# Small float32 products of a block, alternating between tiles of the TensorE array

## The chip, the cores and the metric

The kernel runs on one core of a Trainium2 chip. The core has TensorE (PE), which multiplies, VectorE (DVE), ScalarE (ACT), GpSimd (POOL) and SyncE (SP), whose queue issues most of the transfers from memory. The metric is the time of one execution in device microseconds.

## The reference

Two transformer blocks in float32, one after the other, on 512 tokens of width 1024. The change touches the first block alone:

```python
mod = (silu(c) @ w_ada + b_ada)                 # 1024 x 6144: six vectors, shift, scale and gate of both halves
h = rms_norm(x) * (1 + scale1) + shift1
gq, gk, gv, gz, ga, gb, sq, sk, sv = split(h @ w_in)
# gated delta rule, 8 heads of 64, chunks of 64 tokens
A = where(strict, (kb @ k.T) * decay, 0);  L = A + eye
u, w = solve(L, [v * beta, kb * exp(G)])        # unit lower triangular, 64 x 64
qk = where(causal, (q @ k.T) * decay, 0)
# over the chunks: v_new = u - w S;  o = q_dec S + qk v_new;  S = S * dec + k_dec.T v_new
# sliding window attention, 8 query heads on 2 key heads, window 128, blocks of 128 queries
s = (q @ k.T) / 8 - slope * dist;  p = exp(s - m) / (sum + exp(sink - m));  o = p @ v
x = x + gate1 * (concat(o_g, o_s) @ w_out)
x = x + gate2 * ffn(rms_norm(x) * (1 + scale2) + shift2)
```

## The kernel before

Activations lie transposed, 128 features by 512 tokens in a tile. Large products go through `mm3` (L299): both operands are split into a high and a low part of a faster float32 format, and three products are summed. The small products that the change touches are plain float32, and each is two records of TensorE in the trace. A scheduler sets each engine's order ahead of time; a call under `tc.high_priority` pulls its work forward. On the chip every engine then keeps to its order.

*Modulation.* `w_ada` is read in 16 parts: eight of 256 columns for the first two vectors (`adaln1`, early), eight of 512 (`adaln2`, groups g = 0 to 7) later. `gemv` (L330) makes eight products of a part, the padded vector as weights (32 columns), the matrix as data. The output of product k lies in the 32 partitions from 32 * (k % 4), so four products use four column tiles, and the second four add to the first. `columns` (L337) sums the rows by products with a vector of ones. ADA_AT places the groups: g = 4 and 5 at the turns ADA_AT[2] of the last stage, where their matrix goes through the slots of x4 and x5, two loads of 256 KB at a time (`ring_x`).

*Keys, Gram matrices, inverse.* Heads go by pairs; e, the parity, is the head of the pair that lies in partitions 0 to 63 (e = 0) or 64 to 127. A block b is 128 tokens, two chunks. `key_products` (L729) makes k k^T of four heads of one parity in a PSUM bank, before the stage. `inverse(b)` (a generator of three steps) makes q k^T the same way (L789) and takes the inverse of the 64x64 triangles from inverses of smaller blocks, in two levels; each level is two groups of four products of 128x128x128 (L797 and L802, L811 and L817), with two VectorE operations of 128x512 (L799, L803) or four ScalarE copies behind them. The 128x128 matrices hold two chunks on the diagonal; off it there is nothing that matters.

*Recurrence.* `recur(b)` takes u and w (L857, L862, L865), products with the state (L829), outputs (L893), and the state update (L873), eight products that alternate between two column tiles; `outputs(b)` norms and transposes them (L909).

*Attention.* `swa_scores(b, kv)` makes the scores of four query heads with key head kv (L1005, array rows 64 * kv on), the bias and maximum on VectorE (L1009, L1014), exps (L1021) and scalings (L292) on ScalarE. `swa_values(b, kv)` transposes (L1040), copies (L1042) and multiplies (L1044) into one bank, and ScalarE copies the result into the query tiles x0 to x3 (L1047).

*The order around the change.* The loop over TURNS runs the steps of `inverse`, and after the third `recur` and `outputs`, all under high priority; at each turn n it first calls `swa_step(n)`: the scores of unit n and the values of unit n - 1. Free places on TensorE are filled by products of lower priority, at the end by those of the output projection (`out_proj`, ps_out). The slots x4 and x5, and the others, are loaded again with x for it (L1120), and the result of each group is added to them (L1111), which frees one of three banks.

## Time and profile before

| | us |
|---|---|
| three runs | 1289.23, 1296.19, 1282.57 (median 1289.23) |
| the profiled execution | 1288.95 |
| its span | 1287.2 |
| TensorE busy | 1260.0 (98%) |
| VectorE busy | 788.7 (61%) |
| ScalarE busy | 507.6 (39%) |
| mean granted clock of TensorE | 0.986 |

The span goes from the first to the last instruction. Engines work side by side, so the busy times are no sum. A busy share is an average over stages with different limits; the prediction reads single stages. The granted clock is the share of full speed that the chip gave TensorE; here it stands at 1.0 or at 0.5.

### The profile page before, as it was taken

What the parts mean: (1) busy time and instruction counts of PE and PEld (TensorE: products, weight loads), DVE (VectorE), ACT (ScalarE), POOL (GpSimd) and SP (SyncE); (2) the same over time, 40 slices, a digit from 0 to 9 for tenths busy, and PEclk for the clock granted to TensorE, in tenths of its full rate; (3) what the DMA queues carried; (4) which work ended last, traced back from release to release, by engine and by line L of the source; (5) the groups of instructions that cost most, each with busy time, mean ns of one, the idle gap of its engine ahead of it and who ended that gap; (6) DMA issues with size and microseconds to landing.
All of it is one profiled execution on the core that took longest, in us unless ns stands there. A gap on an engine that the chain in (4) does not pass through costs nothing.

```text
span 1287.2 us, 17346 instructions
## 1 busy us (share of the span) xinstructions
PE 1260.0 (98%) x6670; PEld 1015.7 (79%) x6670; DVE 788.7 (61%) x1665; ACT 507.6 (39%) x988; POOL 42.9 (3%) x39
## 2 busy tenths in 40 slices
PE   5999999999999999999999999999999999999997
PEld 3676778767789888888888888888888888788876
DVE  5598758746565744333433336898778876754554
ACT  4456422635345222222322222345544454432342
POOL 1200001000000000000000000021000000000000
PEclk9999999969999999999999999899999999999999
DMA  9534332002430523232233334122222222233441
GB/s 349 205 106 174 131 99 83 17 17 85 142 119 1 196 85 96 99 98 90 87 101 118 114 119 141 50 75 76 79 82 66 66 78 79 76 96 98 133 145 50
DMA packets 52627, 132.64 MB, mean 103 GB/s; under 512 B 6560, under 2 KB 14272, under 8 KB 52544
## 3 DMA queue, kind: packets, MB, share of 16 engines
q1 hardware_dynamic: 49472, 126.21, 30.4%
q10 hardware_dynamic: 3072, 5.33, 1.3%
q8 instruction: 52, 0.85, 0.3%
q14 instruction: 31, 0.25, 0.1%
HBM read 127.30 MB, written 4.21 MB: 102 GB/s over the span
## 4 chain that ended last, share of the span: by engine, by line
PE 93%; DMA 2%; DVE 2%; ACT 1%; issue 1%; DVEq 0%; ACTq 0%; SPq 0%
PE ps_mm L299 63%; PE ps_out L299 3%; PE ps_sm L330 3%; PE ps_ff L299 2%; PE ps_sc L1538 1%; PE ps_po L1044 1%; PE ps_swa L1005 1%; PE ps_o L1568 1%; DMA raw<-in_wo 1%; PE ps_mm L1683 1%; PE ps_mm L1684 1%; PE ps_tr L1562 1%; PE ps_sc L299 1%; PE ps_mm L1682 1%; PE ps_sm L337 1%; PE ps_g L524 1%
## 5 line engine op out<-in xcount | busy, mean ns | idle before, releaser
L280 ACT ACTIVATE whi<-raw 128x1024 fp32r<-128x1024 f32 x141 | 147.4, 1045 | 275.2 <-PE ps_mm L299 209.3
L281 DVE TENSOR_TENSOR wlo<-raw,whi 128x1024 fp32r<-128x1024 f32 x140 | 170.5, 1218 | 100.5 <-ACT whi L280 100.2
L299 PE MATMUL ps_mm<-uh,whi 128*128 128x512 f32 (+1 forms) x544 | 197.6, 363 | 0.0
L299 PE MATMUL ps_mm<-uh,wlo 128*128 128x512 f32 (+1 forms) x544 | 197.0, 362 | 0.4 <-DVE work L1272 0.4
L299 PE MATMUL ps_mm<-ul,whi 128*128 128x512 f32 (+1 forms) x544 | 195.7, 360 | 0.0
L299 PE MATMUL ps_mm<-mh,whi 128*128 128x512 f32 x320 | 126.3, 395 | 0.0
L299 PE MATMUL ps_mm<-ml,whi 128*128 128x512 f32 x320 | 125.5, 392 | 0.0
L299 PE MATMUL ps_mm<-mh,wlo 128*128 128x512 f32 x320 | 125.2, 392 | 0.0
L299 PEld LDWEIGHTS ps_mm<-ul,whi 128*128 128x128 f32 x544 | 102.8, 189 | 15.7 <-issue 0.7
L299 PEld LDWEIGHTS ps_mm<-uh,whi 128*128 128x128 f32 x544 | 102.6, 189 | 15.7 <-issue 1.5
L299 PEld LDWEIGHTS ps_mm<-uh,wlo 128*128 128x128 f32 x544 | 102.6, 189 | 15.6 <-DVE work L1272 0.7
L299 PEld LDWEIGHTS ps_mm<-ml,whi 128*128 128x128 f32 x320 | 60.0, 188 | 14.2
L299 PEld LDWEIGHTS ps_mm<-mh,wlo 128*128 128x128 f32 x320 | 60.0, 188 | 13.7
L299 PEld LDWEIGHTS ps_mm<-mh,whi 128*128 128x128 f32 x320 | 59.9, 187 | 13.4
L299 PE MATMUL ps_mm<-ah,whi 128*128 128x512 f32 x176 | 69.8, 396 | 0.0
L299 PE MATMUL ps_mm<-al,whi 128*128 128x512 f32 x176 | 69.8, 396 | 0.0
L299 PE MATMUL ps_mm<-ah,wlo 128*128 128x512 f32 x176 | 69.8, 396 | 0.0
L299 PE MATMUL ps_mm<-hh,wlo 128*128 128x512 f32 x144 | 58.3, 405 | 0.0
L299 PE MATMUL ps_mm<-hh,whi 128*128 128x512 f32 x144 | 57.8, 401 | 0.0
L299 PE MATMUL ps_mm<-hl,whi 128*128 128x512 f32 x144 | 57.7, 400 | 0.0
L1186 DVE SCALAR_TENSOR_TENSOR fa<-th,ps_mm 128x512 f32<-128x512 f32 x20 | 13.7, 687 | 58.9 <-ACT th L1184 58.9
L1586 DVE TENSOR_TENSOR work<-ps_mm,rstd 128x512 f32<-128x512 f32 x32 | 22.0, 689 | 45.1 <-PE ps_mm L299 44.9
(559 smaller groups left out, 2418.7 us busy)
## 6 DMA issues: line engine op xcount, KB each, us to landing
raw<-in_win SPq DMA_DIRECT2D x80, 512.0 KB, 3.6
ada<-in_ada SPq DMA_DIRECT2D x48, 256.0 KB, 5.9
raw<-in_wgate SPq DMA_DIRECT2D x22, 512.0 KB, 3.6
raw<-in_wup SPq DMA_DIRECT2D x22, 512.0 KB, 3.5
ada<-in_ada SPq DMA_DIRECT2D x16, 512.0 KB, 4.1
raw<-in_wdown SPq DMA_DIRECT2D x16, 512.0 KB, 3.5
x<-in_xT SPq DMA_DIRECT2D x16, 256.0 KB, 4.0
raw<-in_wout SPq DMA_DIRECT2D x8, 512.0 KB, 3.4
```

Of the source, the lines that this page charges most:

```text
L280: S.activation(out=hi[:, 0:n, :], in_=raw[:, 0:n, :], func=AF.Copy)
L281: eng.tensor_tensor(out=lo[:, 0:n, :], in0=raw[:, 0:n, :], in1=hi[:, 0:n, :].bitcast(F32), op=ALU.subtract)
L299: E.matmul(dst, ww[:, k, :], xx, start=first and i == 0, stop=last and i == len(seq) - 1)
L330: E.matmul(pt[j:j + 32, :], cpad[:, k // 2, k % 2:k % 2 + 32], src, start=k < 4, stop=k >= 4, tile_position=(0, j))
L337: E.matmul(pt[:, j:j + 1], acc[:, j * P:(j + 1) * P], ones[:, 0:1], start=True, stop=True)
L524: E.transpose(dst[:, b * P:(b + 1) * P], src[:, b * P:(b + 1) * P], ident)
L1005: E.matmul(pp[:, f + c0_:f + 256], qsT[j][o:o + 64, b * P:(b + 1) * P], ksT[o:o + 64, k0:(b + 1) * P], start=True, stop=True)
L1044: E.matmul(po_[o:o + 64, :], Vs[:, kblk * P + o:kblk * P + o + 64], pT, start=kb == kbs[0], stop=kb == 1)
L1186: V.scalar_tensor_tensor(out=fa, in0=th, scalar=1.0, in1=pg, op0=ALU.add, op1=ALU.mult)
L1538: E.matmul(pt[:, 0:w], xx[:, sl_], kk[:, c], start=q == 0, stop=q == 2)
L1562: E.transpose(pt[0:nk, i * P:(i + 1) * P], pv(i, c), ident)
L1586: pump(V.tensor_tensor(out=gt, in0=pt, in1=rstd[:, c], op=ALU.mult))
```

## The change

Products that use different parts of the array are put next to each other. In `gemv` the first of each four products also waits for the last load of the four; ADA_AT[2] goes from turns 3 and 6 to 5 and 7, and `ring_x` takes x4, x5 and x6, x7 by turns. Key products and q k^T alternate between the parities, with both banks open. Each 128-wide product of the inverse becomes two 64-wide ones on the diagonal, which alternate; L799 and L803 go by halves. Scores alternate between the key heads, the values of both follow each other, and a turn makes either the scores of a block or its values. Lines of the program move by some twenty: L729 becomes L738, L789 L809, L797 to L817 become L792, L829 L850, L873 L894, L1005 L1026, L1040 L1060, L1044 L1066, L330 L335, L337 L344, L299 L300, L1111 L1136, L1120 L1145, L376 (the loads of `adaln2`) L382.

```diff
-ADA_AT = (2, (3, 4), (3, 6))
+ADA_AT = (2, (3, 4), (5, 7))
...
+    def together(first, last):
+
+        tc.add_manual_dep(first.ins, last.ins.name, SYNC, reason="products side by side")
+
+    def gemv(how, acc, views, loads=()):
 
 
         n = acc.shape[1]
...
         pt = psum("sm")[:, 0:n]
         for k, src in enumerate(views):
             j = 32 * (k % 4)
-            E.matmul(pt[j:j + 32, :], cpad[:, k // 2, k % 2:k % 2 + 32], src, start=k < 4, stop=k >= 4, tile_position=(0, j))
+            ins = E.matmul(pt[j:j + 32, :], cpad[:, k // 2, k % 2:k % 2 + 32], src, start=k < 4, stop=k >= 4, tile_position=(0, j))
+            if k % 4 == 0:
+                together(ins, loads[k // 4])
...
+        views, loads = [], []
         for i in range(4):
             src = A["ada2"][g, i].rearrange("p a b -> p (a b)")
             raws = ring()
             w = 2 * T // len(raws)
             for n, raw in enumerate(raws):
-                nc.sync.dma_start(out=raw, in_=src[:, n * w:(n + 1) * w])
+                ins = nc.sync.dma_start(out=raw, in_=src[:, n * w:(n + 1) * w])
                 views += [raw[:, j:j + T] for j in range(0, w, T)]
+            if i % 2:
+                loads.append(ins)
         acc = accp.tile([P, T], F32, tag="acc", name="acc", bufs=2)
-        gemv(how, acc, views)
+        gemv(how, acc, views, loads)
...
-    def key_products(b, e):
-
-        at = Zf[b, e]
-        o, sl_ = 64 * e, slice(b * P, (b + 1) * P)
+    def key_products(b):
+
+        sl_ = slice(b * P, (b + 1) * P)
         kk = []
 
-        def part(q):
-            if q == 0:
-                kk.append(psum("blk"))
+        def part(q, e):
+            if q + e == 0:
+                kk.extend(psum("blk") for _ in range(2))
                 for i in range(4):
-                    E.matmul(kk[0][:, i * P:(i + 1) * P], kT[i][o:o + 64, sl_], kT[i][o:o + 64, sl_], start=True, stop=True)
+                    for d in range(2):
+                        k_ = kT[i][64 * d:64 * d + 64, sl_]
+                        E.matmul(kk[d][:, i * P:(i + 1) * P], k_, k_, start=True, stop=True)
+            at = Zf[b, e]
...
-        fill.extend(lambda q=q: part(q) for q in range(4))
+        fill.extend(lambda q=q, e=e: part(q, e) for e in range(2) for q in range(4))
...
+        stream = "g" if b == 0 else "inv"
+        ends = (slice(0, 64), slice(64, P))
+
+        def products(dst, left, right):
+
+            for q in range(4):
+                for r in ends:
+                    c = slice(q * P + r.start, q * P + r.stop)
+                    E.matmul(dst[r, c], left[r, c], right[r, c], start=True, stop=True)
+
...
-            qk = psum("g" if b == 0 else "inv")
-            for q in range(4):
-                E.matmul(qk[:, cs[q]], kT[q][o:o + 64, s], qT[q][o:o + 64, s], start=True, stop=True)
-            V.tensor_tensor(out=dt, in0=qk, in1=dt, op=ALU.mult)
+        qk = [psum(stream) for _ in range(2)]
+        for q in range(4):
+            for e in range(2):
+                o = 64 * e
+                E.matmul(qk[e][:, cs[q]], kT[q][o:o + 64, s], qT[q][o:o + 64, s], start=True, stop=True)
+        for e in range(2):
+            dt = qkT[b, e]
+            V.tensor_tensor(out=dt, in0=qk[e], in1=dt, op=ALU.mult)
...
-            pp = psum("g" if b == 0 else "inv")
-            for c in cs:
-                E.matmul(pp[:, c], at[e][:, c], x[e][:, c], start=True, stop=True)
+            pp = psum(stream)
+            products(pp, at[e], x[e])
             pj = tmp_tile(b)
-            V.tensor_tensor(out=a3(pj), in0=a3(pp), in1=bcm(cc("lev", P)), op=ALU.mult)
-            pz = psum("g" if b == 0 else "inv")
-            for c in cs:
-                E.matmul(pz[:, c], pj[:, c], z[:, c], start=True, stop=True)
-            V.tensor_tensor(out=z, in0=z, in1=pz, op=ALU.subtract)
+            for r in ends:
+                V.tensor_tensor(out=a3(pj)[r, :, r], in0=a3(pp)[r, :, r],
+                                in1=bcm(cc("lev", P))[r, :, r], op=ALU.mult)
+            pz = psum(stream)
+            products(pz, pj, z)
+            for r in ends:
+                V.tensor_tensor(out=a3(z)[r, :, r], in0=a3(z)[r, :, r], in1=a3(pz)[r, :, r], op=ALU.subtract)
...
-    def swa_scores(b, kv):
-
-        o = 64 * kv
+    def swa_scores(b):
+
         c0_ = 0 if b else P
-        sc = sw.tile([P, 4, 256], F32, tag="sc", name="sc", bufs=2)
+        sc = [sw.tile([P, 4, 256], F32, tag="sc", name="sc", bufs=2) for _ in range(2)]
+        k0 = (b - 1) * P if b else 0
         for jj in range(2):
-            pp = psum("swa")
+            pp = [psum("swa") for _ in range(2)]
             for j in (2 * jj, 2 * jj + 1):
                 f = (j % 2) * 256
-                k0 = (b - 1) * P if b else 0
-                E.matmul(pp[:, f + c0_:f + 256], qsT[j][o:o + 64, b * P:(b + 1) * P], ksT[o:o + 64, k0:(b + 1) * P],
-                         start=True, stop=True)
+                for kv in range(2):
+                    o = 64 * kv
+                    E.matmul(pp[kv][:, f + c0_:f + 256], qsT[j][o:o + 64, b * P:(b + 1) * P], ksT[o:o + 64, k0:(b + 1) * P],
+                             start=True, stop=True)
...
-    swa_po = [None]
-
-    def swa_values(b, kv, sc):
-        o = 64 * kv
-        if kv == 0:
-            swa_po[0] = psum("po")
-        po_ = swa_po[0]
+    def swa_values(b, sc):
+        po_ = psum("po")
         kbs = (0, 1) if b else (1,)
         for kb in kbs:
-            pp = psum("swa")
-            for j in range(4):
-                E.transpose(pp[:, j * P:(j + 1) * P], sc[:, j, kb * P:(kb + 1) * P], ident)
-            pT = sw.tile([P, T], F32, tag="pT", name="pT", bufs=2)
-            S.activation(out=pT, in_=pp, func=AF.Copy)
-            kblk = b - 1 + kb
-            E.matmul(po_[o:o + 64, :], Vs[:, kblk * P + o:kblk * P + o + 64], pT, start=kb == kbs[0], stop=kb == 1)
-        if kv == 1:
-            for j in range(4):
-                S.activation(out=qsT[j][:, b * P:(b + 1) * P], in_=po_[:, j * P:(j + 1) * P], func=AF.Copy)
-
-    swa_units = [(b, kv) for b in range(NB) for kv in range(2)]
+            pT = []
+            for kv in range(2):
+                pp = psum("swa")
+                for j in range(4):
+                    E.transpose(pp[:, j * P:(j + 1) * P], sc[kv][:, j, kb * P:(kb + 1) * P], ident)
+                pT.append(sw.tile([P, T], F32, tag="pT", name="pT", bufs=2))
+                S.activation(out=pT[kv], in_=pp, func=AF.Copy)
+            for kv in range(2):
+                o = 64 * kv
+                c = (b - 1 + kb) * P + o
+                E.matmul(po_[o:o + 64, :], Vs[:, c:c + 64], pT[kv], start=kb == kbs[0], stop=kb == 1)
+        for j in range(4):
+            S.activation(out=qsT[j][:, b * P:(b + 1) * P], in_=po_[:, j * P:(j + 1) * P], func=AF.Copy)
+
     swa_sc = []
 
     def swa_step(n):
 
-        if n < len(swa_units):
-            swa_sc.append(swa_scores(*swa_units[n]))
-        if n:
-            swa_values(*swa_units[n - 1], swa_sc[n - 1])
+        if n % 2 == 0:
+            swa_sc.append(swa_scores(n // 2))
+        else:
+            swa_values(n // 2, swa_sc[n // 2])
 
...
-    ring_x = lambda: [xtile(4), xtile(5)]
+    ring_n = [0]
+
+    def ring_x():
+        ring_n[0] += 1
+        return [xtile(6), xtile(7)] if ring_n[0] % 2 == 0 else [xtile(4), xtile(5)]
...
-        if n <= len(swa_units):
+        if n < 2 * NB:
```

TensorE's order in the middle of the stage, before. L797 to L817 are groups of the inverse, L1005 scores and L1044 values of the attention, L893 and L873 the recurrence:

```order
L811 MATMUL ps_inv<-h_2177,Z 128x128 x4
L1044 MATMUL ps_po<-pT,Vs 64x512
L1005 MATMUL ps_swa<-ksT,x_1797 128x256
L1005 MATMUL ps_swa<-ksT,x_1853 128x256
L1005 MATMUL ps_swa<-ksT,x_1685 128x256
L1005 MATMUL ps_swa<-ksT,x_1741 128x256
L817 MATMUL ps_inv<-h_2175,blank 128x128 x4
L817 MATMUL ps_inv<-h_2185,blank 128x128 x4
L893 MATMUL ps_so<-vn,qkT 128x64 x8
L873 MATMUL ps_rec<-vn,Kt 64x64 x8
L802 MATMUL ps_inv<-h_2503,l_2789 128x128 x4
```

The same place in the change:

```order
L792 MATMUL ps_inv<-h_2223,blank 64x64 x8
L792 MATMUL ps_inv<-h_2227,blank 64x64 x8
L850 MATMUL ps_rec<-St,kT 128x64 x4
L1066 MATMUL ps_po<-pT,Vs 64x512
L1026 MATMUL ps_swa<-ksT,x_1685 128x256 x2
L1026 MATMUL ps_swa<-ksT,x_1741 128x256 x2
L792 MATMUL ps_inv<-h_2579,l_2885 64x64 x8
L850 MATMUL ps_rec<-St,kT 128x64
L930 MATMUL ps_so<-cst,on 128x128 x4
```

A group of four became one of eight in the same places, scores of a query tile come in pairs (one for each key head), and the values product of this block still stands alone.

TensorE's order at the end of the stage, in the change. L1060 are the transposes of the last attention block, L930 the last of the recurrence, L335 the eight modulation products of g = 5:

```order
L1060 MATMUL ps_swa<-cst,sc 128x128 x4
L930 MATMUL ps_so<-cst,on 128x128 x4
L1066 MATMUL ps_po<-pT,Vs 64x512 x2
L335 MATMUL ps_sm<-x_2843,cpad 32x512
L335 MATMUL ps_sm<-x_2844,cpad 32x512
L335 MATMUL ps_sm<-x_2847,cpad 32x512
L335 MATMUL ps_sm<-x_2848,cpad 32x512
L335 MATMUL ps_sm<-x_2851,cpad 32x512
L335 MATMUL ps_sm<-x_2852,cpad 32x512
L335 MATMUL ps_sm<-x_2855,cpad 32x512
L335 MATMUL ps_sm<-x_2856,cpad 32x512
L344 MATMUL ps_sm<-ones,acc 128x1 x4
```

Before, these eight stood one by one among output products, all of them ahead of the last values products. Now the output products go on behind L344.

SyncE's order there, in the change; x_2851 to x_2856 take the same slots as x_2843 to x_2848, and x_3334 (slot x4) is the first one that the output needs:

```order
L277 DMA raw<-in_wgate 128x1024
L277 DMA raw<-in_wup 128x1024
L382 DMA x_2851<-in_ada 128x512
L382 DMA x_2852<-in_ada 128x512
L382 DMA x_2855<-in_ada 128x512
L382 DMA x_2856<-in_ada 128x512
L1145 DMA x_3330<-in_xT 128x512
L1145 DMA x_3331<-in_xT 128x512
L1145 DMA x_3332<-in_xT 128x512
L1145 DMA x_3333<-in_xT 128x512
L277 DMA raw<-in_wgate 128x1024
L1145 DMA x_3334<-in_xT 128x512
```

Before, the loads of the x tiles were spread over this stretch, two of them among the loads of g = 4; now all of them come behind the last four loads of g = 5.

## Rows read from the trace of the kernel before

**Rows 1.** The page's busy line: engine, us (share of the span), instructions.
```profile
PE 1260.0 (98%) x6670; PEld 1015.7 (79%) x6670; DVE 788.7 (61%) x1665; ACT 507.6 (39%) x988; POOL 42.9 (3%) x39
```

**Rows 2.** Table of stretches: us, busy time (instructions) by engine, granted clock, DMA.
```profile
198.80:367.00 168.20, 166.97 (x1133) 127.17 (x1133) 105.50 (x280) 73.95 (x215) 7.42 (x6) 0.93 0.21 70
...
254.50:278.50 24.00, 23.47 (x108) 15.54 (x108) 11.07 (x33) 5.83 (x14) 0.00 (x0) 0.50 0.00 1
...
250.00:260.00 10.00, 8.97 (x64) 7.16 (x64) 7.89 (x28) 8.17 (x23) 0.00 (x0) 0.73 0.01 2
```

**Rows 3.** TensorE's waits: line, releaser: us in total, times, longest.
```profile
PE ps_sm L330 <- DMA ada<-in_ada: 10.5, 1, 10.5
...
PE ps_out L299 <- DVE x L1111: 1.7, 1, 1.7
...
PE ps_rec L857 <- DVE fs L902: 0.5, 1, 0.5
```

**Rows 4.** TensorE's order of time: start, us, line, records; modulation products.
```profile
88.09 1.07 PE L330 MATMUL ps_sm<-ada,cpad 128*32 128x512 f32 x8
...
330.06 1.05 PE L330 MATMUL ps_sm<-x,cpad 128*32 128x512 f32 x2
```

**Rows 5.** TensorE by line, 190 to 385 us: records | busy us, mean ns.
```profile
L1044 PE MATMUL ps_po<-pT,Vs 128*64 128x512 f32 x28 | 17.0, 710 | 0.0
L1005 PE MATMUL ps_swa<-ksT,x 64*128 64x256 f32 x48 | 14.6, 440 | 0.0
L330 PE MATMUL ps_sm<-x,cpad 128*32 128x512 f32 x32 | 12.1, 604 | 0.0
...
L789 PE MATMUL ps_inv<-qT,kT 64*128 64x128 f32 x48 | 7.1, 286 | 0.0
...
L789 PE MATMUL ps_g<-qT,kT 64*128 64x128 f32 x16 | 2.3, 285 | 0.0
```

**Rows 6.** TensorE by line, 22 to 196 us.
```profile
L330 PE MATMUL ps_sm<-ada,cpad 128*32 128x512 f32 x64 | 14.8, 605 | 0.0
...
L729 PE MATMUL ps_blk<-kT 64*128 64x128 f32 x64 | 7.8, 293 | 0.0
```

**Rows 7.** TensorE's order of time: inverse, state update, 64-wide products, values.
```profile
294.59 1.16 PE L797 MATMUL ps_inv<-l,Z 128*128 128x128 f32 x8
295.58 1.06 PE L817 MATMUL ps_inv<-h,blank 128*128 128x128 f32 x8
...
247.90 0.69 PE L873 MATMUL ps_rec<-vn,Kt 128*64 128x64 f32 x16
248.52 1.16 PE L802 MATMUL ps_inv<-h,l 128*128 128x128 f32 x8
...
309.61 1.02 PE L865 MATMUL ps_rec<-tt,h 64*64 64x64 f32 x14
...
311.85 1.93 PE L1044 MATMUL ps_po<-pT,Vs 128*64 128x512 f32 x4
```

**Rows 8.** TensorE's order of time: products of different array rows.
```profile
284.42 0.27 PE L789 MATMUL ps_inv<-qT,kT 64*128 64x128 f32 x1
284.42 0.27 PE L829 MATMUL ps_rec<-St,kT 64*128 64x64 f32 x1
```

**Rows 9.** VectorE and ScalarE by line, 190 to 370 us.
```profile
L799 DVE TENSOR_TENSOR l<-ps_inv,csta 128x512 f32<-128x512 f32 x6 | 4.1, 677 | 1.9 <-PE ps_inv L797 1.9
...
L831 DVE TENSOR_TENSOR on<-ps_so,egc 128x256 f32<-128x256 f32 x6 | 2.5, 422 | 6.6 <-PE ps_so L829 6.5
...
L1021 ACT ACTIVATE sc<-sc,smx 128x256 f32<-128x256 f32 x24 | 11.9, 497 | 4.6 <-DVE smx L1017 4.5
...
L1047 ACT ACTIVATE x<-ps_po 128x128 f32<-128x128 f32 x16 | 3.1, 284 | 6.9 <-PE ps_po L1044 6.9
```

**Rows 10.** DMA issues: queue, count, KB each, median us from issue to landing.
```profile
x<-in_xT SPq DMA_DIRECT2D x16, 256.0 KB, 4.0
...
x<-in_ada SPq DMA_DIRECT2D x16, 256.0 KB, 2.7
```

More of the change, by code (lines that the diff above doesn't have):

```diff
@@ L356, in ada1_load @@
             t = early.pop(0)
-            nc.sync.dma_start(out=t, in_=A["ada1"][k, i])
-            raws.append(t)
+            raws.append((t, nc.sync.dma_start(out=t, in_=A["ada1"][k, i])))
         return raws
     def adaln1(k, raws):
-        views = [raws[kk // 2][:, kk % 2 * 2 * P:kk % 2 * 2 * P + 2 * P] for kk in range(KD)]
+        views = [raws[kk // 2][0][:, kk % 2 * 2 * P:kk % 2 * 2 * P + 2 * P] for kk in range(KD)]
         acc = accp.tile([P, T], F32, tag="acc", name="acc", bufs=2)[:, 0:2 * P]
-        gemv("E", acc, views)
+        gemv("E", acc, views, [raws[3][1]] * 2)
         columns(acc, k, 8, 2)
     def adaln2(g, how, ring):
-        views = []
+        views, loads = [], []
         for i in range(4):
@@ L808, in inverse @@
             z = a3(Zi[b, e])
-            pp = psum("g" if b == 0 else "inv")
-            for c in cs:
-                E.matmul(pp[:, c], at[e][:, c], x[e][:, c], start=True, stop=True)
+            pp = psum(stream)
+            products(pp, at[e], x[e])
             pj = blank[e]
@@ L814, in inverse @@
                 S.activation(out=a3(pj)[o + 32:o + 64, :, o:o + 32], in_=a3(pp)[o + 32:o + 64, :, o:o + 32], func=AF.Copy)
-            pz = psum("g" if b == 0 else "inv")
-            for c in cs:
-                E.matmul(pz[:, c], pj[:, c], Zi[b, e][:, c], start=True, stop=True)
+            pz = psum(stream)
+            products(pz, pj, Zi[b, e])
             for o in (0, 64):
@@ L939, in build @@
     for b in range(NB):
-        for e in range(2):
-            key_products(b, e)
+        key_products(b)
     rest = [lambda: values(0)] + [lambda p=p, f=f: f(p) for p in range(1, 4) for f in (queries, values)]
@@ new lines, in swa_scores @@
+        for kv in range(2):
+            sm = gs.tile([P, 4, 4], F32, tag="smx", name="smx", bufs=2)
+            mx, es, dn, nm = [sm[:, i, :] for i in range(4)]
+            V.tensor_reduce(out=mx, in_=sc[kv][:, :, c0_:256], axis=AX.X, op=ALU.max)
+            V.tensor_tensor(out=mx, in0=mx, in1=cc("slope", 4, 4 * kv), op=ALU.mult)
+            V.tensor_tensor(out=mx, in0=mx, in1=rows[:, 16 + 4 * kv:20 + 4 * kv], op=ALU.max)
+            V.tensor_scalar(out=nm, in0=mx, scalar1=-1.0, scalar2=None, op0=ALU.mult)
+            V.tensor_tensor(out=es, in0=rows[:, 16 + 4 * kv:20 + 4 * kv], in1=mx, op=ALU.subtract)
+            S.activation(out=es, in_=es, func=AF.Exp)
+            for j in range(4):
+                S.activation(out=sc[kv][:, j, c0_:256], in_=sc[kv][:, j, c0_:256], func=AF.Exp, scale=2.0 ** -(4 * kv + j + 1),
+                             bias=nm[:, j:j + 1], accum_out=dn[:, j:j + 1])
+            V.tensor_tensor(out=dn, in0=dn, in1=es, op=ALU.add)
+            V.reciprocal(out=dn, in_=dn)
+            for j in range(4):
+                scale_by(sc[kv][:, j, c0_:256], dn[:, j:j + 1])
```

35 lines of the change are left out of this document (11 added, 24 removed).

## The prediction, made before the changed kernel ran

> **What bounds the kernel now.** I read the page's busy line first: TensorE 1260.0 of a span of 1287.2 us, 98%, VectorE 61%; the chain of waits then, which runs over TensorE almost throughout [rows 1]. So time comes off only where TensorE has less to do, and it comes off one for one until another engine is late. All that the change touches lies before 385 us; from there on TensorE's order is the same in both kernels. The table of stretches shows the stage that matters, 198.8 to 367.0 us: TensorE busy 166.97 of 168.20, VectorE 105.50, ScalarE 73.95, and inside it 24.00 us at a granted clock of 0.50, the lower of the two levels (1.2 GHz; elsewhere 2.4) [rows 2]. The third row says what TensorE did around the fall: in 250 to 260 it was busy 8.97 of 10.00 [rows 2], among short products, with a wait of 0.5 us on VectorE [rows 3]. The profiled execution took 1288.95 us, 0.3 below the median 1289.23 of the three runs (1282.57 to 1296.19); the sum is made against 1288.95.
>
> **What comes off TensorE.**
>
> (a) *Modulation products.* A group of four products in four 32-wide column tiles already stands side by side in places, and then eight records take 1.07 us; a single product, two records, takes 1.05 [rows 4]. So a group of four costs what one costs. The 96 records of 512 columns are 14.8 and 12.1 us of busy time [rows 5, 6]: 48 products, in the change 12 groups of four. 12 x 1.0 = 12.0, saving 14.9; some of the busy time is a pipelined tail under the next instruction, so I take 14. The 256-column ones at the start wait for their loads (10.5 us in one wait [rows 3]); that they now wait for the last of four I cost at 0, since the loads pace them either way (bounds -1.5 and +1.5).
>
> (b) *Inverse.* A group of four 128-wide products takes 0.99 us from start to start (294.59 to 295.58); 32 groups, 31.7. In the change each is eight 64-wide products, alternating between two tiles. The nearest row is the state update L873, eight such products alternating between two tiles: 247.90 to 248.52, 0.62 for 16 records. 64-wide products in one tile take 1.02 for 14 [rows 7]. 32 x 0.62 = 19.8: saves 11.9. If the two tiles don't overlap, 16 records at 1.02/14 are 1.17, and the term is a loss of 5.8.
>
> (c) *Gram and key products.* 7.1 + 2.3 us (64 records) and 7.8 us (64) [rows 5, 6]. That products of the lower and the upper 64 rows of the array run at once the trace shows: at 284.42 one of either kind starts in the same record time [rows 8]. Halved, that is 8.6 off; groups keep their own switch-over, and I take 6 (bounds 0 and 8.6).
>
> (d) *Attention scores.* 14.6 us for the 48 records of 256 columns [rows 5], some of it at half clock; halved, 7.3 off; I take 5.5, since a pair keeps its switch-over (bounds 0 and 7.3).
>
> (e) *Attention times values.* 28 records, 17.0 us, 14 products [rows 5]. In the new order only three of the seven pairs stand next to each other; the others still have transposes between. A pair saves one product, two records at 0.43 (four of them take 1.93 at 311.85 [rows 7]): 3 x 0.86 = 2.6.
>
> Gross: 14 + 11.9 + 6 + 5.5 + 2.6 = 40.
>
> **What is given back.**
>
> (f) *VectorE in the stage.* Each of 16 inverse operations of 128x512 (677 ns) becomes two of half the partitions and half the elements. The time goes by elements per partition: 128x256 takes 422 ns [rows 9]. So +16 x (0.84 - 0.68) = +2.6 us of VectorE. That alone lay beside TensorE before; the cover shrinks. Of the 40 us about 31 come off this stage (the key products and eight of the twelve groups of (a) lie ahead of it), so TensorE has some 136 us left there against VectorE's 108, and less than that before the tail: 159 output products stood before the last attention product in the old order, 72 do in the new. Two engines that feed each other at such a ratio wait for each other: bounds 0 (all overlaps) and 20 (they take turns in one block of the four after another); I take 5, nearer to the few waits that the trace shows [rows 3] than to the other end.
>
> (g) *The stage's tail.* Before, the last group of modulation products was strung out as singles among output products (as at 330.06), x4 and x5 were reloaded long before use, and one wait of 1.7 us on the output eviction stayed [rows 3]. Now (second pair of orders) its two groups of four stand at the end of the stage with no other product between or behind. Step by step: the transposes of block 3 wait for the exps and scalings of both heads, ScalarE 8 x 0.50 for the exps [rows 9] and as much for scalings of the same shape, 8 us in a row where half of it was before, of which I let 3 show; the first group's bank is that of the values and waits for its four copies, 4 x 0.28 = 1.1 [rows 9]; the second group's loads are issued only once the first group's products have read the slots, 2.7 to landing [rows 10] and the issue of four in a row, which I put at 4.1 together; then the first output product needs a bank that is freed by an eviction on x4, whose reload starts when the second group has read x4: 4.0 [rows 10] plus 0.9 for issue and eviction, less the 2 that the group's end and its columns fill, 2.9. Together 11.1; the old 1.7 goes: 9.4 (bounds 3 and 16, by half or twice the latencies).
>
> (h) *Clock.* The fall to 1.2 GHz costs 12 us now (24.00 us of work at half rate [rows 2]). The change has more short products and more waits, so a fall is as likely as before; I leave it at 12, net 0 (bounds -12, none, and +24, two more of the same length).
>
> **Sum:** 40 - 5 - 9.4 = 25.6 off 1288.95: 1263.4, so about **1264 us**.
>
> **A rule against (b).** No row of before has two tiles of different array rows writing one PSUM bank; L873's tiles differ in columns, the products of [rows 8] go to different banks. The inverse writes both diagonal tiles into one bank, at different partitions. If such writes took turns, (b) would be between 0 and its loss of 5.8, the gross 26, and the time 1288.95 - 26 + 14.4 = 1277. I give it 0.1: in L873 two tiles write one bank at different partitions and overlap [rows 7], and the diagonal tiles also write different partitions. The Trainium skill, TensorEngine Tiling (Array Packing), section Gotcha 1: PSUM Pressure, states that different row tiles cannot use the same PSUM bank at one time; that is the case just worked out, and no row here shows it either way.
>
> **The rivals.**
>
> *VectorE and ScalarE become the bound* (0.18). For it: at most 136 against 108 us in the stage, softmax of both heads at once on ScalarE. If (f) is 15 and (g) 13, the sum is -40 + 28 = 1277; with one more fall of the clock of 6 us, 1283. Against: VectorE's instructions are spread over the stage, and TensorE waits on it for less than 2 us of 168 now. The same page of the Trainium skill, section PSUM Bottleneck, says that faster tiles can leave the PSUM copy as the bottleneck; [rows 2] bear it out only as a possibility.
>
> *More than the sum* (0.18). The tail is covered better than I read (3 instead of 9.4) and (c), (d) reach their halves: 1252; if the clock does not fall in the stage, 1240.
>
> *Slower: the clock* (0.07). It fell near a wait of 0.5 us among short products. The change makes such waits frequent from 200 to 330 us. If the lower level holds most of the stage, 100 us instead of 24, TensorE's work takes 38 us longer again: 1264 + 38 = 1302, and with (f) at 15, 1312. It decides from about 75 us more at half clock. Against: before, the clock came back after 24 us with no other change than that TensorE no longer waited (23.47 us busy of 24.00 [rows 2]).
>
> *It doesn't do what it says* (0.05): alternating products run one after another throughout. Then (a) remains, since [rows 4] has it, (b) is -5.8, (c) to (e) are 0: -14 + 5.8 + 9.4 gives 1290.
>
> **Numbers.** The forecast's own case (1256 to 1272) has 0.42, the one-bank rule 0.10, VectorE and ScalarE 0.18, more 0.18, the clock 0.07, no overlap 0.05. A measurement tells about 1%, 13 us: faster is below 1276, slower above 1302. Faster: 0.42 + 0.18, half of the one-bank case (0.05) and a third of the VectorE case (0.06), 0.71. Slower: the clock case, 0.07. Same: the rest, 0.22. The range takes in the VectorE and the one-bank case above, and of "more" all but the case without a fall of the clock: 1245 to 1287.
>
> **What would show it.** (b): the products of L792 start in pairs, a group in about 0.62 us; 1.0 or more says the one-bank rule. (a): groups of eight L335 records in 1.0. (c), (d): two records of L809 or L1026 in the time of one. (f): TensorE's busy share from 200 to 330 us, now above 0.98, at 0.95 or so, with VectorE as the releaser; below 0.88 is the rival. (g): waits of TensorE on x<-in_ada (about 4 us) and on the eviction L1136 (about 3) just after the last values product. (h): one stretch of about 24 us at 0.50, no more. The prediction is wrong if the order that both kernels share after 385 us starts less than 15 or more than 40 us earlier.

## The result, and the profile after

The changed kernel takes 1295.68 us (median of 19 runs, 1289.88 to 1301.86) against 1288.66 before (19 runs): a ratio of 1.0061, 95% interval 1.0044 to 1.0078. It is 0.6% slower, less than the 1% that the prediction took as no change, and outside its range of 1245 to 1287. Runs over 1.5% above the fastest of their kernel, two of inv_serial and one of no_swa below, are left out of the ratios.

The page of the changed kernel; its busy line answers to [rows 1], and the last line is the granted clock in 40 slices.

```profile
span 1291.6 us, 17879 instructions
...
PE 1236.5 (96%) x6926; PEld 1007.6 (78%) x6926; DVE 789.8 (61%) x1681; ACT 507.4 (39%) x988; POOL 42.5 (3%) x39
...
PEclk9999998779889999999999999899999999999999
```

TensorE is busy 23.5 us less and the span is 4.4 longer. The table of stretches of the changed kernel (us, then busy time of PE, PEld, DVE, ACT, POOL, granted clock, DMA), with the stretch that also stands for the experiments in the first row:

```profile
200.00:340.00 140.00, 122.40 (x1182) 96.70 (x1177) 97.73 (x261) 65.27 (x197) 6.18 (x6) 0.83 0.19 61
...
210.00:220.00 10.00, 6.59 (x119) 6.23 (x121) 9.00 (x27) 3.73 (x18) 0.00 (x0) 0.84 0.28 80
240.00:250.00 10.00, 5.85 (x46) 5.21 (x44) 8.78 (x23) 1.73 (x8) 0.00 (x0) 0.71 0.01 2
250.00:260.00 10.00, 7.61 (x63) 6.85 (x62) 3.61 (x10) 7.31 (x23) 0.00 (x0) 0.50 0.00 0
290.00:300.00 10.00, 7.70 (x114) 7.12 (x114) 8.32 (x27) 8.03 (x29) 0.00 (x0) 0.83 0.20 54
```

The same stretch before:

```profile
200.00:340.00 140.00, 138.77 (x929) 104.88 (x928) 91.27 (x242) 64.78 (x196) 7.42 (x6) 0.91 0.19 60
```

Where TensorE stands at 6 to 8 of 10 us, VectorE stands at 8 to 9, or ScalarE at 7 to 8: TensorE waits by turns for either. Its waits in the changed kernel, the largest of 200 to 340 us (before, none in this stretch was over 0.5 us [rows 3]):

```profile
PE ps_so L850 <- DVE on L852: 3.9, 1, 3.9
PE ps_inv L883 <- ACT work L880: 3.1, 2, 2.4
PE ps_inv L792 <- DVE smx L1040: 2.8, 1, 2.8
PE ps_inv L792 <- DVE l L821: 1.9, 1, 1.9
```

One of them in the order of time, ScalarE of the changed kernel: the exps of both heads stand in a row, the first four at 248.27 and four more from 250.35, and the copy L880 behind the last.

```profile
248.27 0.51 ACT L1044 ACTIVATE sc<-sc,smx 128x256 f32<-128x256 f32 x1 [11.60 <-DVE smx L1040]
...
251.92 0.50 ACT L1044 ACTIVATE sc<-sc,smx 128x256 f32<-128x256 f32 x1
252.32 0.20 ACT L1044 ACTIVATION_READ_ACCUMULATOR sc<-sc,smx 128x1 f32 x1
252.41 0.58 ACT L880 ACTIVATE work<-ps_rec 64x512 f32<-64x512 f32 x1
```

And TensorE behind it, then the end of the stage: the last values, the two groups of g = 5, their columns, the first output product. In brackets what TensorE waited for.

```profile
253.04 1.97 PE L883 MATMUL ps_inv<-work,Z 64*64 64x64 f32 x16 [2.39 <-ACT work L880]
...
343.77 1.45 PE L1066 MATMUL ps_po<-pT,Vs 128*64 128x512 f32 x4
346.36 1.06 PE L335 MATMUL ps_sm<-x,cpad 128*32 128x512 f32 x8 [1.13 <-ACT x L1068]
353.98 1.94 PE L335 MATMUL ps_sm<-x,cpad 128*32 128x512 f32 x8 [6.56 <-DMA x<-in_ada]
356.71 1.86 PE L344 MATMUL ps_sm<-ones,acc 128*128 128x1 f32 x8 [0.79 <-ACT acc L338]
360.27 0.58 PE L300 MATMUL ps_out<-mh,kept 128*128 128x256 f32 x1 [1.70 <-DVE x L1136]
```

**The account.** For TensorE's part up to the first product of the feed-forward block (396.95 us before, 399.75 after) I counted, from its first record on, the time of each record to the next one's start, up to its own duration, as work, and the rest as idle; what lies in a stretch at half clock counts as half work and half loss. At the very start the profile names no lower clock, yet 16 modulation records of 256 columns take 1.93 us there and 1.07 from about 22 us on (from 36 us in turns and gemv_gram57); that time counts as work. By kinds, in us:

| | before | after | foreseen |
|---|---|---|---|
| modulation, 512 columns | 25.2 | 12.1 | -14 |
| modulation, 256 columns | 14.7 | 11.0 | 0 |
| inverse | 31.9 | 19.1 | -11.9 |
| key products and q k^T | 15.6 | 13.9 | -6 |
| scores | 13.7 | 9.4 | -5.5 |
| values | 13.4 | 11.8 | -2.6 |
| all work at full clock | 367.8 | 327.9 | -40 |
| loss to half clock | 11.7 | 27.8 | 0 |
| idle | 7.0 | 32.8 | +14.4 |

The work fell by 39.9 us, and 40 were foreseen; that the sums agree is luck, since the five terms of the forecast came to 33.5, the 256-column products to 3.7, and 2.7 lie in products that the change does not touch. Idle time rose by 25.8 and the loss to the clock by 16.1: 41.9 against 39.9.

### The profile page after: what moved, and what is told of

Same layout as the page of the kernel before. It is cut to its first block, busy times and chain, and to the rows that moved or that the text cites. A ratio compares the mean times of both kernels' runs of the same rounds, so it can differ in the third digit from the quotient of the medians.

```text
span 1291.6 us, 17879 instructions
## 1 busy us (share of the span) xinstructions
PE 1236.5 (96%) x6926; PEld 1007.6 (78%) x6926; DVE 789.8 (61%) x1681; ACT 507.4 (39%) x988; POOL 42.5 (3%) x39
## 4 chain that ended last, share of the span: by engine, by line
PE 86%; DVE 6%; ACT 4%; DMA 3%; issue 1%; SPq 0%; DVEq 0%; ACTq 0%
PE ps_mm L300 62%; PE ps_out L300 4%; PE ps_ff L300 2%; PE ps_sm L335 2%; PE ps_sc L1563 1%; PE ps_o L1593 1%; DMA raw<-in_wo 1%; PE ps_po L1066 1%; PE ps_tr L1587 1%; ACT sc L1044 1%; PE ps_sc L300 1%; PE ps_mm L1708 1%; PE ps_mm L1707 1%; PE ps_mm L1709 1%; PE ps_swa L1060 1%
## 5 line engine op out<-in xcount | busy, mean ns | idle before, releaser
L300 PE MATMUL ps_mm<-uh,wlo 128*128 128x512 f32 (+1 forms) x544 | 197.0, 362 | 0.8 <-DVE work L1297 0.4
L300 PE MATMUL ps_mm<-uh,whi 128*128 128x512 f32 (+1 forms) x544 | 197.5, 363 | 0.0
L300 PE MATMUL ps_mm<-ul,whi 128*128 128x512 f32 (+1 forms) x544 | 195.6, 360 | 0.0
L300 PE MATMUL ps_mm<-mh,whi 128*128 128x512 f32 x320 | 126.3, 395 | 0.0
L300 PE MATMUL ps_mm<-ml,whi 128*128 128x512 f32 x320 | 125.5, 392 | 0.0
L300 PE MATMUL ps_mm<-mh,wlo 128*128 128x512 f32 x320 | 125.2, 392 | 0.0
L300 PEld LDWEIGHTS ps_mm<-uh,wlo 128*128 128x128 f32 x544 | 102.4, 188 | 16.5 <-DVE wlo L282 0.8
L300 PEld LDWEIGHTS ps_mm<-ul,whi 128*128 128x128 f32 x544 | 102.7, 189 | 15.7 <-issue 0.7
L300 PEld LDWEIGHTS ps_mm<-uh,whi 128*128 128x128 f32 x544 | 102.5, 188 | 15.7 <-issue 1.5
L300 PEld LDWEIGHTS ps_mm<-ml,whi 128*128 128x128 f32 x320 | 60.0, 188 | 14.2
L300 PEld LDWEIGHTS ps_mm<-mh,wlo 128*128 128x128 f32 x320 | 60.0, 188 | 13.8
L300 PEld LDWEIGHTS ps_mm<-mh,whi 128*128 128x128 f32 x320 | 59.9, 187 | 13.4
L300 PE MATMUL ps_mm<-ah,whi 128*128 128x512 f32 x176 | 69.8, 396 | 0.0
L300 PE MATMUL ps_mm<-al,whi 128*128 128x512 f32 x176 | 69.8, 396 | 0.0
L300 PE MATMUL ps_mm<-ah,wlo 128*128 128x512 f32 x176 | 69.8, 396 | 0.0
L300 PE MATMUL ps_mm<-hh,whi 128*128 128x512 f32 x144 | 58.1, 403 | 0.0
L300 PE MATMUL ps_mm<-hl,whi 128*128 128x512 f32 x144 | 57.9, 402 | 0.0
L300 PE MATMUL ps_mm<-hh,wlo 128*128 128x512 f32 x144 | 57.9, 402 | 0.0
L1211 DVE SCALAR_TENSOR_TENSOR fa<-th,ps_mm 128x512 f32<-128x512 f32 x20 | 13.7, 687 | 58.8 <-ACT th L1209 58.8
```

Of the source, the lines that this page charges most:

```text
L300: E.matmul(dst, ww[:, k, :], xx, start=first and i == 0, stop=last and i == len(seq) - 1)
L1211: V.scalar_tensor_tensor(out=fa, in0=th, scalar=1.0, in1=pg, op0=ALU.add, op1=ALU.mult)
```

## The experiments

Ratios are to the kernel before on the same chip, with 95% intervals; the clock is the mean granted clock of the runs that the ratio rests on, the lowest and the highest. The last three columns are the account above for one execution, the profiled one.

| kernel | ratio | interval | runs | clock | work | clock loss | idle |
|---|---|---|---|---|---|---|---|
| before | 1 | |  | 0.986 to 0.990 | 367.8 | 11.7 | 7.0 |
| the change | 1.0061 | 1.0044 to 1.0078 | 19 | 0.960 to 0.971 | 327.9 | 27.8 | 32.8 |
| turns | 1.0045 | 1.0030 to 1.0060 | 8 | 0.967 to 0.972 | 334.1 | 27.0 | 27.6 |
| gemv_alone | 0.9878 | 0.9857 to 0.9899 | 5 | 0.986 to 0.993 | 348.4 | 9.5 | 8.4 |
| inv_alone | 1.0060 | 1.0036 to 1.0083 | 7 | 0.972 to 0.979 | 354.9 | 28.9 | 8.8 |
| swa_alone | 1.0076 | 1.0046 to 1.0105 | 6 | 0.984 to 0.989 | 369.5 | 9.3 | 12.7 |
| inv_serial | 1.0126 | 1.0071 to 1.0181 | 2 | 0.967 to 0.977 | 363.4 | 27.3 | 7.1 |
| gemv_inv | 0.9877 | 0.9850 to 0.9904 | 4 | 0.975 to 0.981 | 335.9 | 20.5 | 10.0 |
| gemv_gram | 0.9828 | 0.9802 to 0.9854 | 5 | 0.992 to 0.995 | 347.8 | 5.1 | 8.0 |
| no_swa | 0.9877 | 0.9820 to 0.9934 | 3 | 0.968 to 0.985 | 334.9 | 19.9 | 10.2 |
| swa_turns | 1.0065 | 1.0043 to 1.0086 | 6 | 0.986 to 0.990 | 369.5 | 10.8 | 11.1 |
| dve_split | 0.9936 | 0.9915 to 0.9958 | 9 | 0.992 to 0.999 | 368.1 | 1.7 | 4.5 |
| inv_first | 0.9826 | 0.9790 to 0.9861 | 6 | 0.985 to 0.996 | 344.3 | 8.5 | 10.2 |
| gemv_gram57 | 0.9919 | 0.9895 to 0.9944 | 4 | 0.985 to 0.990 | 354.5 | 6.9 | 12.0 |
| gemv_gram_swa | 0.9840 | 0.9814 to 0.9867 | 4 | 0.989 to 0.992 | 344.7 | 5.9 | 8.1 |

The clock column says how far one execution stands for the rest. The profiled execution of the kernel before is at the low end of its runs (0.986), that of the change near the high end (0.970, median 0.965), so in most pairs of runs the clock differs by more than in the account. From the medians, 0.965 and 0.989, I estimate 91 us at half clock in the whole kernel against 28. The six kernels with the inverse 64 wide in all blocks lie at 0.985 and below, the others at 0.984 and above.

**Turns back** (turns), the changed kernel with one number put back:

```diff
-ADA_AT = (2, (3, 4), (5, 7))
+ADA_AT = (2, (3, 4), (3, 6))
```

> The changed kernel with one number put back: the late modulation groups at turns 3 and 6 as before, not 5 and 7; all the rest of the change stays. Its order has output products between and behind the second group again. Theory A (the tail lost it): of the changed kernel's tail, 12.2 us of waits and some 7 us of work at half clock behind 330 us go, so 15 to 19 us faster than the changed kernel, about 1277 to 1281, and under 4 us of waits after the last group. Rival B (VectorE and the clock in 206 to 330 us lost it, 15.6 us of waits and 38 us of work at half clock, and what leaves the tail only comes back there): within 5 us of the changed kernel, 1290 or more.

By the ratios it is 2 us faster than the change, by the medians 4, and the intervals overlap: the rival's forecast held. In the account 5 us of idle time go and 6 us of work come back. Of that work 5.1 us lie ahead of 62 us, in the longer slow start of this execution; the 512-column groups take 14.0 instead of 12.1, two of them broken up again. The output evictions now make TensorE wait 9.0 us. The tail is not where most of the time went.

**Modulation alone** (gemv_alone), the kernel before with `together`, the loads and `ring_x` of the change:

```diff
+            if k % 4 == 0:
+                together(ins, loads[k // 4])
...
-    ring_x = lambda: [xtile(4), xtile(5)]
+        return [xtile(6), xtile(7)] if ring_n[0] % 2 == 0 else [xtile(4), xtile(5)]
```

> The kernel before with the modulation part alone: four products side by side behind the last of their loads, four slots in turn, turns 3 and 6 as before. Theory A: the products need no VectorE, so their saving stays whole, 12 to 14 us: 1275 to 1277. Rival B (every us saved on TensorE in the stage comes back as a wait or as clock): the eight groups ahead of the stage save 7 to 8, the rest is lost: 1281 or more.

1.2% faster, 15.7 us: the saving stays whole. The account gives 19.4 us of work, 10.3 of it in the 512-column products and 4.3 in the 256-column ones, that the prediction put at nothing. But of the 5.5 us by which the work of the first 61 us fell, the clock and waits took back 3.6 there.

**Inverse alone** (inv_alone), the kernel before with:

```diff
-                E.matmul(pp[:, c], at[e][:, c], x[e][:, c], start=True, stop=True)
+            products(pp, at[e], x[e])
...
+                V.tensor_tensor(out=a3(z)[r, :, r], in0=a3(z)[r, :, r], in1=a3(pz)[r, :, r], op=ALU.subtract)
```

> The kernel before with the inverse alone in 64-wide products. Both theories have the groups at about 0.62 us and 12 us less of TensorE's work. Theory A (tail): there is no new tail here, so 8 to 12 us faster, 1277 to 1281. Rival B: the work that goes is that which kept TensorE busy while VectorE and ScalarE did theirs; waits rise by 5 or more, the time at half clock from 24 to 35 us or more, and the time is within 4 us of before, 1285 to 1289.

The rival's sign, and more than it said: 0.6% slower with 12.9 us less work. The groups do stand side by side; TensorE of this kernel in the order of time, at full clock:

```profile
216.97 0.68 PE L782 MATMUL ps_g<-x,work 64*64 64x64 f32 x16
217.49 0.40 PE L782 MATMUL ps_g<-x,Z 64*64 64x64 f32 x8
217.72 0.63 PE L782 MATMUL ps_inv<-h,Z 64*64 64x64 f32 x16
218.19 0.40 PE L782 MATMUL ps_g<-x,Z 64*64 64x64 f32 x8
```

16 records in 0.52 us, from 216.97 to 217.49. Idle time is up by only 1.8 us. What takes the gain is one stretch of 58 us at half clock, where before it was 24 [rows 2]; the table of stretches of this kernel:

```profile
224.80:282.80 58.00, 57.71 (x349) 43.09 (x345) 31.96 (x87) 22.69 (x78) 2.14 (x2) 0.50 0.05 15
```

TensorE is busy in 57.71 of the 58.00 us; it is not waiting that holds the clock down here. One wait of 1.3 us stands just ahead of the fall. All seven runs have a lower clock than any run of the kernel before, 0.972 to 0.979 against 0.986 to 0.990.

**The same products, not side by side** (inv_serial), against the kernel above:

```diff
-            for q in range(4):
-                for r in ends:
+            for r in ends:
+                for q in range(4):
```

> The kernel before with the inverse in 64-wide products that are not alternated: four in one diagonal tile, then four in the other. The products are those of the inverse alone, only their order differs, so a group should take about 1.0 us again, as long as one of 128-wide products, and TensorE is as busy as before. Theory C (the clock falls with what of the array a product uses): the clock stays at half for 45 us or more, as in the inverse alone (58 us), and the time is 1296 or more. Rival D (the clock falls because side-by-side products leave TensorE short of work): half clock for about 24 us, as before, and a time within 4 us of the kernel before.

As theory C had it, the clock stays down nearly as long (54.6 us in the stage), with 7.1 us idle as before, and the kernel is 1.3% slower, by two runs; the profiled one is the faster. Two of its four stretches at half clock:

```profile
255.60:279.50 23.90, 23.90 (x92) 15.68 (x90) 12.04 (x27) 6.77 (x18) 0.00 (x0) 0.50 0.00 1
228.30:245.40 17.10, 17.10 (x121) 12.99 (x120) 10.17 (x24) 7.90 (x30) 2.14 (x2) 0.50 0.09 26
```

So the fall needs no alternation, and no more waiting than before. The other two stretches, from 310.2 and from 327.3 us, begin when TensorE has had no wait over 0.15 us since 255 us. A group cost 27.5/32 = 0.86 us, less than the 1.0 expected: products at the end of one group still ran beside the first of the next.

**VectorE's operations split, products left wide** (dve_split), the kernel before with:

```diff
-            V.tensor_tensor(out=a3(pj), in0=a3(pp), in1=bcm(cc("lev", P)), op=ALU.mult)
+            for h in (slice(0, 2), slice(2, 4)):
+                V.tensor_tensor(out=a3(pj)[:, h, :], in0=a3(pp)[:, h, :], in1=bcm(cc("lev", P))[:, h, :], op=ALU.mult)
...
+            for h in (slice(0, 256), slice(256, T)):
+                V.tensor_tensor(out=z[:, h], in0=z[:, h], in1=pz[:, h], op=ALU.subtract)
```

> A control: the kernel before with the two VectorE operations of each inverse step in halves of 128x256, so that VectorE has the added 2.6 us of the inverse part, while TensorE's products stay 128 wide. Theory C (the clock follows the products): half clock for 17 to 31 us in the stage and a time within 4 us of before. If the split operations on VectorE are what drew the clock down in the inverse alone: 45 us or more at half clock and 1294 or more.

So VectorE operations in halves, the other side of inv_alone's edit, do not lower the clock; these are halves by columns, 128x256, those of inv_alone 64x256, of the same 0.42 us. Against both theories the clock rose: the fall of [rows 2] is gone but for 3.4 us, all nine runs are at 0.992 or above, and the kernel is 0.64% faster with the same work. The stretch of [rows 2] in this kernel:

```profile
254.50:278.50 24.00, 23.91 (x179) 18.19 (x177) 18.45 (x56) 14.22 (x46) 0.00 (x0) 0.97 0.14 45
```

The scheduler placed the products a little differently around the split operations, and TensorE waits 0.43 us in the whole stage instead of 2.9. A fall of 24 us thus hangs on little; together with the 2.5 us less of waiting it is worth 0.6%.

**Modulation and inverse** (gemv_inv; the two edits above together):

> Modulation part and inverse part together, attention and Gram part as before. Theory C/B (what the inverse saves is taken by the clock): slower than the modulation part alone although TensorE has 12 us less to do; 1272 to 1282, with 40 us or more at half clock in the stage. Rival A (each saving on TensorE counts once the tail is sound): 1258 to 1262.

Nearly as theory C had it, and not as rival A: not slower than the modulation alone, but at the same ratio, though there are 12.5 us less of work; 11.0 us go to the clock (37.5 us at half clock in the stage) and 1.6 to waits.

**Modulation, key and Gram products** (gemv_gram), the second edit being

```diff
+        for q in range(4):
+            for e in range(2):
+                o = 64 * e
+                E.matmul(qk[e][:, cs[q]], kT[q][o:o + 64, s], qT[q][o:o + 64, s], start=True, stop=True)
```

and the same in `key_products`:

> Modulation part with the key and Gram part. In the order of the changed kernel the products of the two parities stand mostly one bank after the other and not alternating, and its key and Gram products took 13.9 us against 15.6 before. So no more than 2 us from the modulation part alone, 1268 to 1272. If the prediction's term of 6 us were right for this order, 1264.

1.7% faster, 1264.79 us. That is the time which the term of 6 us would give, but not by that term: key and Gram products fell by 1.0 us against the modulation alone, work in all by 0.6. The rest of the difference lies in the clock (4.4), and the intervals nearly touch.

**All but the attention, and all but the inverse** (no_swa; gemv_gram_swa), both with turns 3 and 6; the edits are those of the change without `swa_scores` and `swa_values`, and without `products`.

> The whole change without the attention part, late modulation groups at turns 3 and 6: modulation, key and Gram products, inverse. If the attention part is what costs (its new waits, softmax of both heads at once), 1272 to 1280, most of the way to the modulation part alone. If inverse and clock are, about the same as the change with turns 3 and 6, 1288 to 1292.

> Modulation, key and Gram part with the attention part, the inverse left 128 wide, turns 3 and 6. It is the fourth corner beside modulation and Gram (0.983 of before), with the inverse (0.988) and with the inverse and the attention (1.0045). If the attention part costs by itself what it costs alone, 9 us: 1273 to 1277 (0.990) with 30 us or less at half clock in the stage, and the two parts then add up to some 8 us more together than apart. If it costs the 21 us of the full change here too, without the inverse: 1284 to 1288 and 12 us of waits or more above those of modulation and Gram.

With gemv_gram and turns they make a square:

| ratio (idle, clock loss in us) | attention as before | attention of the change |
|---|---|---|
| inverse 128 wide | 0.983 (8.0, 5.1) | 0.984 (8.1, 5.9) |
| inverse 64 wide | 0.988 (10.2, 19.9) | 1.0045 (27.6, 27.0) |

no_swa took what its first expectation gives, by three runs: beside the 64-wide inverse it is the attention part that costs. Neither expectation held for gemv_gram_swa: without the 64-wide inverse the attention part costs nothing here, neither 9 nor 21 us. The stretch from 200 to 340 us in the four corners: gemv_gram, gemv_gram_swa and no_swa,

```profile
200.00:340.00 140.00, 138.59 (x1054) 111.25 (x1053) 96.94 (x250) 70.94 (x212) 7.39 (x6) 0.99 0.25 79
200.00:340.00 140.00, 136.66 (x1064) 107.86 (x1062) 94.81 (x249) 71.34 (x211) 7.59 (x6) 0.99 0.26 82
200.00:340.00 140.00, 134.66 (x1247) 102.60 (x1248) 97.80 (x254) 69.03 (x208) 6.62 (x6) 0.87 0.24 77
```

and turns, which differs from gemv_gram_swa by the inverse alone:

```profile
200.00:340.00 140.00, 124.63 (x1215) 99.69 (x1217) 95.93 (x249) 59.64 (x175) 6.88 (x6) 0.83 0.21 67
```

Taking the 64-wide inverse out of that kernel makes it 2% faster (1.0045 to 0.984), although it gives TensorE 10.6 us more to do.

**Attention alone, and its order of turns alone** (swa_alone; swa_turns), the kernel before with the attention part, and with this much of it:

```diff
+        for u in (n - n % 2, n - n % 2 + 1):
+            if n % 2 == 0:
+                swa_sc.append(swa_scores(*swa_units[u]))
+            else:
+                swa_values(*swa_units[u], swa_sc[u])
```

> The kernel before with the attention part alone: score products of both key heads alternating, one turn for scores and the next for values. Theory A: 5 to 8 us less of TensorE's work, 4 to 8 us faster: 1281 to 1285. Rival B: the softmax of a block now lies between its scores and its values with no scores of another unit beside it; new waits eat the saving, within 3 us of before.

> The kernel before with the order of the attention turns alone: one turn makes the scores of both key heads of a block, the next its values; the products themselves and their order within a head stay as before, none is put side by side. If the turn order (softmax of both heads in one run of VectorE and ScalarE, no scores beside the values) is what cost the attention part its time, waits of TensorE in the stage rise by 4 us or more and the time is 6 us or more over before, 1294 or more. If the alternating products themselves do it (by the clock or their banks), within 3 us of before.

Both are slower by the same, 0.7 to 0.8%: on the stage of the kernel before it is the order of the turns that costs, with 4 to 6 us more of idle time. That is what swa_turns was to tell by 1294 us or more; for swa_alone neither expectation had so much. The largest wait of each in the stage, of swa_alone and then of swa_turns (before, at most 0.5 us [rows 3]):

```profile
PE ps_rec L857 <- DVE smx L1018: 3.4, 1, 3.4
PE ps_rec L857 <- DVE rsy L397: 3.5, 1, 3.5
```

The alternation itself saved 1.1 us of scores and 0.4 of values there, and the late modulation groups lost 1.4. Not all of the 8 us is in the profiled execution of swa_turns (4.9 by the first product of the feed-forward block). It is the fastest of its six runs (1290.75 us, median 1296.19) and has the highest clock, 0.990; the other five are at 0.986 or 0.987.

**The inverse 64 wide in block 0 alone** (inv_first), added to gemv_gram:

```diff
-        ends = (slice(0, 64), slice(64, P))
+        ends = (slice(0, 64), slice(64, P)) if b == 0 else (slice(0, P),)
```

> Modulation, key and Gram part, and the inverse in 64-wide alternating products for block 0 alone, whose groups stand among the 512-column products of the projections; blocks 1 to 3 keep 128-wide ones. Theory C: among wide products the clock holds, so these 8 groups save 8 x 0.4 = 3.2 us: 1260 to 1264, with under 15 us at half clock in the stage. If 64-wide products draw the clock down wherever they stand: 30 us or more at half clock, 1270 or more.

The eight groups take 4.7 us instead of 7.4, and in the profiled execution the clock mostly holds (10.2 us at half clock in the stage, against 3.4 in gemv_gram). It does not in every run: four of the six took 1259 to 1263 us at a clock of 0.992 to 0.996, two took 1272.6 at 0.985 and 0.988. In time there is no difference from gemv_gram that the intervals show, and whether 64-wide groups are harmless among wide products stays open.

**Late turns on a sound stage** (gemv_gram57), gemv_gram with turns 5 and 7:

> Modulation, key and Gram part with the late modulation groups at turns 5 and 7, as in the change. In its order both groups of g = 5 stand behind the last values products here too, but the stage's other products keep TensorE busier. Theory A (the tail by itself costs 10 us or more): 1273 or more, with waits of 6 us or more on the loads and on the output eviction. If the tail only waits because the stage is empty: within 3 us of turns 3 and 6, 1262 to 1268.

0.9% slower than gemv_gram, 12 us, with the waits that theory A named: 3.3 us on the loads, 3.2 on the eviction.

```profile
PE ps_sm L335 <- DMA x<-in_ada: 3.3, 2, 2.2
PE ps_out L300 <- DVE x L1127: 3.2, 1, 3.2
```

TensorE's order is the same in both up to 277 us, where the profiled executions are 2.5 us apart; at the first product of the feed-forward block they are 13.0 apart. So the late turns cost some 10 us by themselves: behind 277 us there are 6.8 us more of idle time and 3.5 more of clock loss. Of the 6.7 us more of work in the table 6.5 lie ahead of 63 us, in the longer slow start of this execution.

## Why the prediction was wrong

The range was missed at its upper end and the sign was wrong; its sum failed in two terms of the second half, (h) and (f). The order that both kernels share, which was to start 15 to 40 us earlier, starts 2.8 us later.

- **(a)** held: 13.1 us for 14. The work of the 256-column products, put at 0 with a bound of 1.5, fell by 3.7 more; in time the 0 held, since the 101st record of the first projections starts at 62.0 us before and at 60.9 in the change, and over all kernels at 60.6 to 62.8 with the old early part and at 60.4 to 62.9 with the new.
- **(b)** held: 12.8 us for 11.9. The one-bank rule is out: the diagonal tiles write one bank at different partitions and 16 records take 0.52 us. The Trainium skill, TensorEngine Tiling (Array Packing), section Gotcha 1: PSUM Pressure, excludes two row tiles in one bank at one time; this measurement does not agree for tiles that write different partitions of it, and it decides.
- **(c)** was 1.7 for 6. The mechanism is right: where the two parities alternate, as in key products at 86.10 and 88.54 us, their records start 6 to 7 ns apart, and q k^T of block 0 went from 2.2 to 1.1 us. But the order has most groups one bank after the other, as at 208.72, where eight records start 111 ns apart; that could have been read from it. TensorE of the changed kernel:

```profile
208.72 1.05 PE L809 MATMUL ps_inv<-qT,kT 64*128 64x128 f32 x8
```

- **(d), (e)** came to 4.3 for 5.5 and 1.6 for 2.6: right mechanism, and pairs that the order breaks up.
- **(g)** held in size. From 330.01 us on TensorE idled 12.2 us, for 11.1 foreseen before the 1.7 was taken off; 6.6 of it is the load of the second group (4.1 foreseen), 1.7 the eviction (2.9), 1.7 the transposes (3). What it left out is that a fall of the clock comes with these waits, 20.5 us at half clock between 336 and 364 us; gemv_gram57, with late turns too, has 10.2 us there and gemv_gram none.
- **(f)** was put at 5 us. From 206.6 to 330.0 us TensorE idled 15.6, 14.4 more than in the stage before, and its busy share from 200 to 330 us fell to 0.88 (114.37 of 130 us), the edge that was to tell of the rival. The square shows why the price could not be read from one part: the inverse or the attention alone adds 0 to 2 us of idle time to gemv_gram, both together 19.6. It is not the amount of work alone: no_swa has as little for TensorE in all as turns (334.9 and 334.1 us) and idles 10.2 against 27.6. It takes the bursts of the new turns (both heads' softmax at once) and the shorter products; that the shorter products no longer fill these bursts is my reading, no run shows it by itself. The prediction's sum of what is left, 136 us against 108, asked for the amount only. (Its 159 output products stand before the last transposes of the recurrence; before the last attention product there are 146.) The rival "VectorE and ScalarE become the bound" fits in size, net 14.4 for its 15 and 10.5 for its 13, but with the clock on top.
- **(h)** is the step that failed worst: "I leave it at 12, net 0". It cost 16 us more in the profiled execution. The inverse alone shows it nearly free of everything else: 12.9 us of work gained, 17.2 lost to the clock, 1.8 more idle. The prediction looked for the cause in waits and gave the clock 0.07, at 75 us more of half clock; it was 41 us more in the profiled execution (64.9 in the stage for 23.9), some 62 by the estimate from the medians, and the waits did the rest. Its argument against, that the clock came back once TensorE no longer waited, fails in inv_alone, where TensorE is busy 57.71 of 58.00 us at half clock. What sets the fall is not shown as a rule. Shown is that 64-wide products in place of 128-wide ones bring it, alternated or not (inv_alone, inv_serial), in all six kernels that have them in all blocks, and that VectorE operations in halves don't (dve_split); with 64-wide groups in block 0 alone the clock was lower in two runs of six (inv_first).

What stays open: why dve_split's order is spared the fall that the kernel before has, which of the products of the stage tip it, and why the attention part costs 0.8% on the kernel before and nothing on gemv_gram.

The best kernels of the study are the change with turns 3 and 6 and without its inverse (gemv_gram_swa, 1262.98 us, 0.984), without inverse and attention (gemv_gram, 1264.79 us, 0.983), and the latter with the inverse of block 0 (inv_first, 1262.23 us, 0.983), 1.6 to 1.7% faster than before; they don't differ by the intervals.

## What to carry to other kernels

Putting small products side by side pays at once where the products feed nothing urgent, as the modulation's; where they are one end of a chain over VectorE and ScalarE, try the parts together and not only one by one, since the price can come when the last part goes in: here 0 to 2 us of waits for either part, 19.6 for both. Before a product is cut to use less of the array, see whether the granted clock already falls in its stretch: here a cut that saved 13 us of work lost 17 to the clock. Read the clock of all runs and not of the profiled one alone. And read from the order itself whether products that the code alternates do stand next to each other.

## What the runs showed of the hardware that was not expected

TensorE stayed at half clock for 58 us in a stretch in which it was busy nearly all the time (57.71 us at 0.50), and the clock also fell with no wait over 0.15 us in the 55 us ahead (inv_serial, 310.2 us). A fall can come or not by a small change of order: 24 us at half clock before, 3.4 with two VectorE operations split, together with 2.5 us less of waiting worth 0.64% of the whole kernel. And two 64x64 tiles on the diagonal, in one PSUM bank, take 0.52 us for 16 records, where four 128-wide products take 0.99 [rows 7].
